# SSD scan of a two-layer hybrid backbone: decay tiles apart from their loads, convolutions written one tile ahead, other buffers in the first gates

## Chip, cores, metric

One Trainium2 chip; the kernel runs on one core. The metric is the time of one execution in device microseconds, the median of the runs shown.

## What is computed

Two layers over 1024 latent and 256 context tokens of width 1024: first a bidirectional Mamba-2 SSD mixer, then grouped-query attention, each followed by an expert-choice mixture of 16 SwiGLU experts. All inputs are float32. The change lies in the SSD mixer. What matters of it, from the reference:

```python
z, xbc, dtr = jnp.split(u @ in_w, [D_INNER, D_INNER + CONV_DIM], axis=-1)
xbc = jax.nn.silu(dwconv_centred(xbc, conv_w, conv_b))          # width 5, then x, B, C
dt = jax.nn.softplus(dtr.reshape(b, L, 2, SSD_HEADS) + dt_bias)
# per direction, chunks of 128 tokens, a = dt * A, acum = cumsum(a) in the chunk
seg = jnp.exp(jnp.where(tri, acum[..., :, None] - acum[..., None, :], -jnp.inf))
cb = jnp.einsum('bclgn,bcsgn->bcgls', Cc, Bc)                   # 8 groups, state size 128
y_diag = jnp.einsum('bcgrls,bcsgrp->bclgrp', cb[:, :, :, None] * seg, xdt)
states = jnp.einsum('bcsgn,bcgrs,bcsgrp->bcgrpn', Bc, decay_end, xdt)
# h[c+1] = chunk_decay[c] * h[c] + states[c]
y_off = jnp.einsum('bclgn,bcgrpn,bcgrl->bclgrp', Cc, h_prev, jnp.exp(acum))
y = y_f + flip(y_b) + D_skip * xs
out = rmsnorm(y * silu(z), norm_w) @ out_w
```

## The kernel before, in words

Work stands with channels on the 128 partitions and the 1280 tokens (10 chunks of 128, the first two are context) along the free dimension. Products of the projections are made from high and low halves of both factors (`mm3`, L51: three matmuls, L54 to L56).

The scan stage of `ssd` (from L303) runs over 8 groups (L501). A group has one B tile, one C tile and two x tiles of 128 channels (two heads each). Each of these is made by `conv_tile` (L333): the weights are fetched and split (`weights`, L306: the DMA on SP at L309, the high half on ACT at L311, the low half on POOL at L314), 72 projection matmuls of 256 or 512 columns go to `in_ps` (`proj`, L319, three PSUM buffers), ACT moves them out (L344, L345), and DVE makes the width-5 convolution and SiLU with four passes over 1284 columns (L349) and two over 642 (L354), with a tanh on ACT between them (L353). `cb` is the product of B and C by chunk (L513, moved out by ACT at L514). `transposed` (L357) turns B and x by chunk on PE (L363).

`core` (L384) is called for each of the two x tiles of a group (L519). It runs the backward states H1 (weighted x L370, matmul L396, the step on DVE L382), and then goes over five pairs of chunks. In round i of its loop pair i gets its `decays` (L403), that is the tile `Eb` with the log decays of both directions and heads (a DMA of 512 KB issued by SP at L405), masked by POOL (L408, two per pair), put through exp by ACT (L413, eight per pair); POOL adds the two directions in place (L416), DVE multiplies by `cb` (L417), and the result M is a view of the first half of `Eb`. `Eb` has three buffers. The same round takes pair i a step forward (`forward`, L420: L429, L382), makes the entering part of pair i-1 (`entering`, L435: matmuls L442, scaling on DVE L451, sum of directions on POOL L452, result `yos`), and the output of pair i-2 (`output`, L455: L460 with M, L463 with `yos`, both into `y_ps`; then L467 on DVE and the DMA of y to memory at L469).

Behind the scan the output gates follow: `gate` (L471) projects z for 128 channels, loads y back (L489) and multiplies (L490 to L492), writes the product (L493) and adds its squares (L499). The first two of sixteen (`early`, L524) are written while the pools of the scan are still held and take their tiles from `halves` (L529), two pairs out of the four quarters of one tile; the others take them from `pair` (L547).

The order of each engine's instructions is not that of the source. A scheduler takes the program as written, gives earlier written work precedence, and at each step places what its own estimate says is ready; buffers set when a tile can be used again. So the place at which a call stands sets how early its work may be placed, and work of a later tile fills what an earlier one leaves open.

## Time and profile before

| what | value |
|---|---|
| median of 3 runs (lowest to highest) | 3840.92 us (3840.58 to 3845.42) |
| the profiled execution, its own time | 3852.41 us |
| its span in the trace | 3850.6 us |
| PE busy (TensorE matmuls) | 3562.8 us, 93% |
| DVE / ACT / POOL busy | 2594.0 / 2024.8 / 1811.8 us |
| mean granted TensorE clock | 0.973 |

The span is divided by stage: the scan with its projections from about 142 to 992 us, the other gates and the output projection up to about 1470 us, the first mixture of experts, attention, the second mixture. PE is an engine whose work is pipelined, so that a busy stretch of it need not be PE at its peak; idle time of it and what ended it is read in the groups by line. In the rows, L12 is line 12 of the kernel before, `out<-in` are tiles, "128x512 f32<-128x512 f32" the shapes, and "x640" how many. The matmuls with float32 operands that the kernel writes as one stand as two instructions in the trace.

### The profile page before, as it was taken

The page shows a single profiled execution, that of the slowest core. Times are in us where ns is not written, and L with a number is a line of the kernel's source. Part 1 is how long each engine was busy: PE and PEld are TensorE (multiplying, and loading weights), DVE is VectorE, ACT ScalarE, POOL GpSimd, SP SyncE. Part 2 cuts the span into 40 slices and gives each one's busy share as a digit, 9 for nine tenths or more (in the row PEclk, how much of TensorE's full clock was granted, in tenths as well). Part 3 has the DMA queues.
Part 4 walks back from the last instruction along what each step waited for, and adds up shares of the span by engine and source line. Part 5 has one row for each costly group of instructions (what it writes and reads, how often), then busy time and mean ns, then how long its engine had stood idle before and what let it go on. Part 6 is the DMA issues. An engine that isn't in the chain of part 4 may idle for free.

```text
span 3850.6 us, 56599 instructions
## 1 busy us (share of the span) xinstructions
PE 3562.8 (93%) x21156; PEld 2674.7 (69%) x21156; DVE 2594.0 (67%) x3675; ACT 2024.8 (53%) x3310; POOL 1811.8 (47%) x1356
## 2 busy tenths in 40 slices
PE   6999999999898998999999998899999976999997
...
GB/s 191 108 104 116 128 90 83 79 77 90 161 137 142 119 117 244 315 305 311 319 320 304 287 238 91 39 17 1 1 1 12 118 168 265 371 382 379 343 339 163
DMA packets 296803, 681.10 MB, mean 177 GB/s; under 512 B 22568, under 2 KB 148400, under 8 KB 290384
## 3 DMA queue, kind: packets, MB, share of 16 engines
...
## 4 chain that ended last, share of the span: by engine, by line
PE 37%; DVE 11%; issue 6%; DMA 5%; POOL 4%; ACT 2%; SPq 0%; ACTq 0%; POOLq 0%; DVEq 0%
DVE m_w L728 6%; PE pv L1177 5%; PE S L1143 4%; PE a_tr L1164 4%; PE acc L54 4%; PE acc L56 4%; PE acc L55 4%; POOL m_w L725 3%; PE cacc L695 3%; DMA m_raw<-in_moe_w_dram 3%; PE o_ps L55 1%; PE o_ps L56 1%; PE o_ps L54 1%; PE qkv L56 1%; PE qkv L54 1%
## 5 line engine op out<-in xcount | busy, mean ns | idle before, releaser
L728 DVE TENSOR_TENSOR m_w<-m_raw,m_w 128x1792 fp32r<-128x1792 f32 (+1 forms) x384 | 890.5, 2342 | 251.8 <-ACT m_w L722 249.5
L722 ACT ACTIVATE m_w<-m_raw 128x2048 fp32r<-128x2048 f32 x384 | 732.6, 1916 | 485.9 <-DMA m_raw<-in_moe_w_dram 268.1
L725 POOL TENSOR_TENSOR m_w<-m_raw,m_w 128x256 fp32r<-128x256 f32 (+1 forms) x384 | 824.7, 2175 | 346.1 <-ACT m_w L722 343.5
L54 PE MATMUL in_ps<-hh,w 128*128 128x512 f32 (+1 forms) x1152 | 423.6, 368 | 7.7 <-DVE th L491 7.7
L55 PE MATMUL acc<-m_w,xl 128*128 128x512 f32 x1024 | 407.9, 399 | 22.3 <-DVE m_w L728 13.7
L56 PE MATMUL in_ps<-hh,w 128*128 128x512 f32 (+1 forms) x1152 | 420.7, 365 | 0.0
L55 PE MATMUL in_ps<-hl,w 128*128 128x512 f32 (+1 forms) x1152 | 418.7, 363 | 0.0
L54 PE MATMUL acc<-m_w,xl 128*128 128x512 f32 x1024 | 407.2, 404 | 4.5 <-ACT xl L48 4.5
L56 PE MATMUL acc<-m_w,xl 128*128 128x512 f32 x1024 | 402.1, 393 | 0.0
L413 ACT ACTIVATE Eb<-Eb,ebias 128x128 f32<-128x128 f32 x640 | 199.4, 391 | 165.2 <-POOL Eb L408 163.5
L1147 DVE TENSOR_REDUCE mx<-S 128x1 f32<-128x1024 f32 x128 | 155.7, 1216 | 181.2 <-PE S L1143 179.2
L1194 POOL TENSOR_TENSOR q<-s 64x128 f32<-64x128 f32 x128 | 58.7, 459 | 415.2 <-DVE mx L1152 347.4
L55 PEld LDWEIGHTS acc<-m_w,xl 128*128 128x128 f32 x1024 | 193.9, 189 | 83.9 <-DVE m_w L728 28.8
L54 PEld LDWEIGHTS in_ps<-hh,w 128*128 128x128 f32 x1152 | 220.1, 191 | 45.4 <-issue 10.9
L54 PEld LDWEIGHTS acc<-m_w,xl 128*128 128x128 f32 x1024 | 193.5, 190 | 69.6 <-issue 21.4
L56 PEld LDWEIGHTS in_ps<-hh,w 128*128 128x128 f32 x1152 | 220.0, 191 | 31.1 <-issue 5.0
L55 PEld LDWEIGHTS in_ps<-hl,w 128*128 128x128 f32 x1152 | 219.8, 191 | 29.2 <-issue 3.7
L314 POOL TENSOR_TENSOR w<-w_raw,w 128x512 fp32r<-128x512 f32 x96 | 154.5, 1630 | 166.4 <-ACT w L311 156.0
L56 PEld LDWEIGHTS acc<-m_w,xl 128*128 128x128 f32 x1024 | 193.7, 189 | 38.4 <-DVE xl L49 0.2
L55 PE MATMUL acc<-m_w,gT 128*128 128x512 f32 x512 | 204.4, 399 | 6.6 <-DVE m_w L728 4.1
L54 PE MATMUL acc<-m_w,gT 128*128 128x512 f32 x512 | 202.7, 402 | 1.0 <-ACT gT L48 1.0
L56 PE MATMUL acc<-m_w,gT 128*128 128x512 f32 x512 | 203.1, 397 | 0.0
...
## 6 DMA issues: line engine op xcount, KB each, us to landing
m_raw<-in_moe_w_dram SPq DMA_DIRECT2D x384, 1024.0 KB
...
```

What stands on the lines that cost most here:

```text
L54: mm(out, lhs[0], rhs[0], start=start, stop=False)
L55: mm(out, lhs[0], rhs[1], start=False, stop=False)
L56: mm(out, lhs[1], rhs[0], start=False, stop=stop)
L314: nc.gpsimd.tensor_tensor(w[1][:, sl], raw[:, sl], w[0][:, sl].bitcast(F32), op=OP.subtract)
L413: nc.scalar.activation(Eb[:, d, hh, cc], Eb[:, d, hh, cc], AF.Exp, bias=bias[:, c0 + cc, k:k + 1])
L722: nc.scalar.activation(w[0], raw, AF.Copy)
L725: nc.gpsimd.tensor_tensor(w[1][:, :, n:], raw[:, :, n:], w[0][:, :, n:].bitcast(F32), op=OP.subtract)
L728: nc.vector.tensor_tensor(w[1][:, :, :n], raw[:, :, :n], w[0][:, :, :n].bitcast(F32), op=OP.subtract)
L1143: nc.tensor.matmul(o, qTs[self.qt][:, 2 * self.hp + hh], kT[k][:, self.kv, 512 * b:512 * b + n], start=(k == 0), stop=(k == 1))
L1147: nc.vector.tensor_reduce(self.mx[:, 0:1], S[hh], axis=AX.X, op=OP.max)
L1164: nc.tensor.transpose(ps[:, q], self.pr[hh][:, (c0 + q) * P:(c0 + q + 1) * P], net.ident)
L1177: nc.tensor.matmul(self.pv[o:o + 64, 0], v32[:, t, self.kv], self.PT[:, t], start=(t < 2), stop=(t >= NT - 2))
```

## The change

- `decays` writes the sum of the two directions into a tile of its own, M, with three buffers, and `Eb` has two buffers in place of three.
- The calls are written in another order. `tile_BC` and `tile_x` hold the two kinds of convolution tile. B and C of group g+1 are written between the two cores of group g; both x tiles of a group are written ahead of its first core.
- The first two gates turn through all four quarters of one tile for y (`halves`), and take `th` from the buffers `raw` of the convolution.
- The 128x128 matrix of ones and the two triangles move from constants that are held all the time into the pool of the dt stage; the triangles are made by a memset and two affine selects on POOL in place of two comparisons on DVE. A column of ones stays.

```diff
--- before.py
+++ after.py
@@ -60,8 +60,7 @@
         nc, tc, A = self.nc, self.tc, self.A
         cp = self.cp = es.enter_context(tc.tile_pool(name="consts", bufs=1))
         self.ident = cp.tile([P, P], F32, name="ident")
-        self.tri = cp.tile([P, 2, P], F32, name="tri")
-        self.ones = cp.tile([P, P], F32, name="ones")
+        self.ones = cp.tile([P, 1], F32, name="ones")
         nc.vector.memset(self.ones, 1.0)
         self.eps = cp.tile([P, 1], F32, name="eps")
         nc.vector.memset(self.eps, EPS)
@@ -78,8 +77,6 @@
             nc.gpsimd.iota(jp, pattern=[[1, P]], base=0, channel_multiplier=-1,
                            allow_small_or_imprecise_dtypes=True)
             nc.vector.tensor_scalar(self.ident, jp, 0.0, None, op0=OP.is_equal)
-            nc.vector.tensor_scalar(self.tri[:, 0], jp, 0.0, None, op0=OP.is_ge)
-            nc.vector.tensor_scalar(self.tri[:, 1], jp, 0.0, None, op0=OP.is_le)
 
             r0 = pr.tile([P, P], F32, name="r0")
             r1 = pr.tile([P, P], F32, name="r1")
@@ -227,6 +224,13 @@
 
 
         with tc.tile_pool(name="dtp", bufs=1) as dp, tc.tile_pool(name="dtps", bufs=1, space=PSUM) as pp:
+            ones = dp.tile([P, P], F32, name="ones_pp")
+            tri = dp.tile([P, 2, P], F32, name="tri")
+            nc.vector.memset(ones, 1.0)
+            nc.vector.memset(tri, 1.0)
+            for d, sg in ((0, 1), (1, -1)):
+                nc.gpsimd.affine_select(tri[:, d], tri[:, d], pattern=[[sg, P]], base=0, channel_multiplier=-sg,
+                                        compare_op=OP.is_ge, fill=0.0)
             wdt = wp.tile([P, KT, P], F32, name="w_raw")
             nc.scalar.dma_start(wdt[:, :, 0:64], wv[:, :, 6144:6208])
             wdh = wp.tile([P, KT, 2, 64], F32R, name="w0")
@@ -279,9 +283,9 @@
             for d in range(2):
                 dsl = slice(32 * d, 32 * d + 32)
                 fps = pp.tile([P, NT, 32], F32, name="fps")
-                nc.tensor.matmul(fps, self.tri[:, d], a[:, :, dsl], start=True, stop=True)
+                nc.tensor.matmul(fps, tri[:, d], a[:, :, dsl], start=True, stop=True)
                 tps = pp.tile([P, NT, 32], F32, name="tps")
-                nc.tensor.matmul(tps, self.ones, a[:, :, dsl], start=True, stop=True)
+                nc.tensor.matmul(tps, ones, a[:, :, dsl], start=True, stop=True)
                 nc.vector.tensor_tensor(bias[:, :, dsl], ld[:, :, dsl], fps, op=OP.subtract)
                 nc.scalar.activation(eF[:, :, dsl], fps, AF.Exp)
                 fsb = dp.tile([P, NT, 32], F32, name="fsb")
@@ -293,7 +297,7 @@
             fr = dp.tile([64, NT, P], F32, name="fr")
             for t in range(NT):
                 rp = pp.tile([64, 2, P], F32, name="rps")
-                nc.tensor.matmul(rp, a[:, t, :], self.tri, start=True, stop=True)
+                nc.tensor.matmul(rp, a[:, t, :], tri, start=True, stop=True)
                 for d in range(2):
                     nc.scalar.activation(fr[32 * d:32 * d + 32, t], rp[32 * d:32 * d + 32, d], AF.Copy)
             for d in range(2):
@@ -401,7 +405,7 @@
             state = [None]
 
             def decays(c0):
-                Eb = co.tile([P, 2, 2, 2, P], F32, name="Eb", bufs=3)
+                Eb = co.tile([P, 2, 2, 2, P], F32, name="Eb", bufs=2)
                 nc.sync.dma_start(Eb.rearrange("p d h c l -> p (d h) (c l)"),
                                   rows(fd, [0, P], [TOK, 4], [1, 256], off=4 * ct * TOK + c0 * P))
                 for d, sg in ((0, 1), (1, -1)):
@@ -412,8 +416,8 @@
                             k = 32 * d + 2 * ct + hh
                             nc.scalar.activation(Eb[:, d, hh, cc], Eb[:, d, hh, cc], AF.Exp,
                                                  bias=bias[:, c0 + cc, k:k + 1])
-                M = Eb[:, 0]
-                nc.gpsimd.tensor_tensor(M, M, Eb[:, 1], op=OP.add)
+                M = co.tile([P, 2, 2, P], F32, name="M", bufs=3)
+                nc.gpsimd.tensor_tensor(M, Eb[:, 0], Eb[:, 1], op=OP.add)
                 nc.vector.tensor_tensor(M, M, cb[:, None, c0:c0 + 2].to_broadcast([P, 2, 2, P]), op=OP.mult)
                 return M
 
@@ -498,11 +502,22 @@
                     nc.scalar.activation(th[:, :n], yd[:, :n], AF.Square)
                     nc.gpsimd.tensor_tensor(acc[:, t0:t0 + n], first[:, t0:t0 + n], th[:, :n], op=OP.add)
 
-        for g in range(NG):
+        def tile_BC(g):
             BT = hp.tile([P, PTOK], F32, name="BT", tag="h_lo")
             CT = gp.tile([P, PTOK], F32, name="CT", bufs=2)
             conv_tile(16 + g, BT)
             conv_tile(24 + g, CT)
+            return BT, CT
+
+        def tile_x(ct):
+            xT = gp.tile([P, PTOK], F32, name="xT", bufs=2)
+            conv_tile(ct, xT)
+            return xT
+
+        BC = tile_BC(0)
+        for g in range(NG):
+            BT, CT = BC
+            xT = [tile_x(2 * g)]
             Btm = transposed(BT, "Btm", gp)
             cb = gp.tile([P, NT, P], F32, name="cb")
             for c0 in range(0, NT, 4):
@@ -512,10 +527,11 @@
                     sl = at(c0 + q)
                     nc.tensor.matmul(ps[:, q], BT[:, sl], CT[:, sl], start=True, stop=True)
                 nc.scalar.activation(cb[:, c0:c0 + n], ps[:, :n], AF.Copy)
-            for h in range(2):
-                xT = gp.tile([P, PTOK], F32, name="xT", bufs=2)
-                conv_tile(2 * g + h, xT)
-                core(2 * g + h, xT, CT, Btm, cb)
+            xT.append(tile_x(2 * g + 1))
+            core(2 * g, xT[0], CT, Btm, cb)
+            if g + 1 < NG:
+                BC = tile_BC(g + 1)
+            core(2 * g + 1, xT[1], CT, Btm, cb)
         for _ in mods:
             pass
 
@@ -526,8 +542,8 @@
 
         def halves():
             nonlocal turns
-            turns ^= 2
-            return zt[:, turns], zt[:, turns + 1]
+            turns = (turns + 1) % 4
+            return zt[:, turns], gp.tile([P, 1288], F32, name="raw", bufs=2)[:, :512]
         for ct in range(early):
             gate(ct, weights(ct * P), pin, halves, acc0, acc0 if ct else None)
         for p_ in (pst, ptp, pin, co, gp, adp, cs):
@@ -610,7 +626,7 @@
                     if t == NCT and h == 0:
                         ssp = pp.tile([P, NT], F32, name="r_lg")
                         for u in range(NT):
-                            nc.tensor.matmul(ssp[:, u:u + 1], self.acc[:, u * P:(u + 1) * P], self.ones[:, 0:1],
+                            nc.tensor.matmul(ssp[:, u:u + 1], self.acc[:, u * P:(u + 1) * P], self.ones,
                                              start=True, stop=True)
                         nc.scalar.activation(yr, ssp, AF.Sqrt, bias=self.eps, scale=1.0 / DI)
                         nc.vector.reciprocal(yr, yr)
```

What the scheduler makes of it is shown at three places. In the changed kernel the lines of `core` stand four later (L460 is L464, L463 is L467, L442 is L446, L417 is L421, L408 is L412, L382 is L386, L370 is L374, L349 is L353, L354 is L358, L452 is L456), the sum of directions is L420, and the matmul of cb L528.

First, PE at the fourth and fifth pair of a core's outputs in the steady part. Before:

```order
L442 MATMUL yo_ps<-H_7469,CT 128x128
L442 MATMUL yo_ps<-H_7254,CT 128x128
L55 MATMUL in_ps<-hl,w_7905 128x512
L56 MATMUL in_ps<-hh,w_7906 128x512
L54 MATMUL in_ps<-hh,w_7905 128x512
L55 MATMUL in_ps<-hl,w_7905 128x512
L56 MATMUL in_ps<-hh,w_7906 128x512
L54 MATMUL in_ps<-hh,w_7905 128x512
L55 MATMUL in_ps<-hl,w_7905 128x512
L460 MATMUL y_ps<-Eb,xtm 64x128 x2
L463 MATMUL y_ps<-ident,yos 128x128
```

and with the change, from the fourth pair's output to the fifth's:

```order
L467 MATMUL y_ps<-ident,yos 128x128
L367 MATMUL tr_ps<-ident,BT 128x128 x4
L54 MATMUL in_ps<-hh,w_5275 128x256
L55 MATMUL in_ps<-hl,w_5275 128x256
L56 MATMUL in_ps<-hh,w_5276 128x256
L464 MATMUL y_ps<-M,xtm 64x128 x2
L54 MATMUL in_ps<-hh,w_5275 128x256
L55 MATMUL in_ps<-hl,w_5275 128x256
L367 MATMUL tr_ps<-ident,BT 128x128 x2
L56 MATMUL in_ps<-hh,w_5276 128x256
L54 MATMUL in_ps<-hh,w_5275 128x256
L467 MATMUL y_ps<-ident,yos 128x128
```

Seven projections of 512 columns stood ahead of the fourth pair's output (and six ahead of the fifth's); now there are fewer and narrower ones, and the next group's B is turned between them.

Second, DVE around the convolution of C. Before:

```order
L349 SCALAR_TENSOR_TENSOR CT<-raw,pcol,CT 128x1284 x3
L354 SCALAR_TENSOR_TENSOR CT<-raw,CT 128x642 x2
L417 TENSOR_TENSOR Eb<-Eb,cb 128x512 x3
L349 SCALAR_TENSOR_TENSOR xT<-raw,pcol,xT 128x1284 x4
L354 SCALAR_TENSOR_TENSOR xT<-raw,xT 128x642 x2
L370 TENSOR_TENSOR xw_5247<-xtm,wst 128x256
```

and with the change:

```order
L353 SCALAR_TENSOR_TENSOR CT<-raw,pcol,CT 128x1284
L374 TENSOR_TENSOR xw_6896<-xtm,wst 128x256
L353 SCALAR_TENSOR_TENSOR CT<-raw,pcol,CT 128x1284
L382 COPY H_6895<-st_ps 128x128
L353 SCALAR_TENSOR_TENSOR CT<-raw,pcol,CT 128x1284
L386 SCALAR_TENSOR_TENSOR H_6895<-H_6895,dec,st_ps 128x64
L353 SCALAR_TENSOR_TENSOR CT<-raw,pcol,CT 128x1284
L386 SCALAR_TENSOR_TENSOR H_6895<-H_6895,dec,st_ps 128x64
L374 TENSOR_TENSOR xw_6904<-xtm,wst 128x512
L358 SCALAR_TENSOR_TENSOR CT<-raw,CT 128x642 x2
L386 SCALAR_TENSOR_TENSOR H_6895<-H_6895,dec,st_ps 128x64 x8
L374 TENSOR_TENSOR xw_6919<-xtm,wst 128x384
```

The C that stood right ahead of its use (cb, and through it L417) is now the C of the next group, between the backward states of this group's second core.

Third, POOL through a core's pairs (tiles yos, Eb and M). Before:

```order
L452 TENSOR_TENSOR yos<-yos 128x2x128 x2
L416 TENSOR_TENSOR Eb<-Eb 128x512
L408 AFFINE_SELECT Eb<-Eb 128x512 x4
L416 TENSOR_TENSOR Eb<-Eb 128x512
L452 TENSOR_TENSOR yos<-yos 128x2x128
```

and with the change:

```order
L456 TENSOR_TENSOR yos<-yos 128x2x128
L412 AFFINE_SELECT Eb<-Eb 128x512
L456 TENSOR_TENSOR yos<-yos 128x2x128
L412 AFFINE_SELECT Eb<-Eb 128x512 x3
L420 TENSOR_TENSOR M<-Eb 128x512
L456 TENSOR_TENSOR yos<-yos 128x2x128
```

The masks between the sums of yos are those of the next core's pairs now, and the last sum of yos of a core stands behind three of them and one sum into M.

## Rows read from the trace of the kernel before

**Rows 1.** The page of the profiled execution, its first part (busy time and share of the span of each engine) and the row of its second part for PE (40 slices of 96 us, busy share in tenths).

```profile
PE 3562.8 (93%) x21156; PEld 2674.7 (69%) x21156; DVE 2594.0 (67%) x3675; ACT 2024.8 (53%) x3310; POOL 1811.8 (47%) x1356
...
PE   6999999999898998999999998899999976999997
```

**Rows 2.** Busy time by window, us (number of instructions in brackets), for the whole scan stage and for one of its eight groups, from one group's first x transpose to the next one's; behind the engines the granted TensorE clock, the share of the DMA engines and GB/s.

```profile
142.00:992.00 850.00, 789.54 (x4804) 621.17 (x4804) 607.61 (x1130) 406.03 (x1012) 420.25 (x477) 0.99 0.32 101
705.00:811.50 106.50, 99.22 (x607) 80.40 (x605) 76.96 (x141) 52.04 (x129) 52.80 (x62) 0.98 0.26 82
```

**Rows 3.** Groups of PE instructions in the window 142 to 992 us: busy us, mean ns of one | idle time of PE before them and what ended it.

```profile
L442 PE MATMUL yo_ps<-H,CT 128*128 128x128 f32 x576 | 90.4, 279 | 0.2 <-DVE yos L451 0.2
L460 PE MATMUL y_ps<-Eb,xtm 128*64 128x128 f32 x640 | 86.3, 299 | 37.8 <-DVE Eb L417 18.2 <-issue 16.9 <-ACT Eb L413 1.8
L463 PE MATMUL y_ps<-ident,yos 128*128 128x128 f32 x320 | 74.8, 316 | 0.7 <-POOL yos L452 0.7
L429 PE MATMUL st_ps<-xw,Btm 128*128 128x128 f32 x288 | 59.0, 286 | 2.8 <-DVE H L382 2.3 <-DVE H L378 0.4
...
L363 PE MATMUL tr_ps<-ident,xT 128*128 128x128 f32 x160 | 27.8, 291 | 8.5 <-DVE xT L354 8.4
...
L513 PE MATMUL tr_ps<-CT,BT 128*128 128x128 f32 x140 | 20.3, 284 | 9.7 <-DVE CT L354 9.7
```

**Rows 4.** PE in order of time, the rows of that same group that have idle time before them (start, us, what, idle before it and its releaser).

```profile
777.58 0.44 PE L460 MATMUL y_ps<-Eb,xtm 128*64 128x128 f32 x4 [1.62 <-issue]
...
792.76 1.16 PE L513 MATMUL tr_ps<-CT,BT 128*128 128x128 f32 x8 [1.60 <-DVE CT L354]
...
811.08 0.63 PE L363 MATMUL tr_ps<-ident,xT 128*128 128x128 f32 x4 [0.99 <-DVE xT L354]
```

**Rows 5.** All engines in order of time, from the first pair's y of one core to the fourth pair's (SPq issues DMAs; rows of other work left out).

```profile
760.83 0.44 PE L460 MATMUL y_ps<-Eb,xtm 128*64 128x128 f32 x4
...
761.31 0.37 SPq L405 DMA_DIRECT2D Eb<-fd  x1
...
764.90 1.23 POOL L408 TENSOR_SCALAR_AFFINE_SELECT Eb<-Eb 128x512 f32<-128x512 f32 x2 [2.04 <-DMA Eb<-fd]
...
765.58 2.45 ACT L413 ACTIVATE Eb<-Eb,ebias 128x128 f32<-128x128 f32 x8 [2.12 <-POOL Eb L408]
...
768.52 0.72 POOL L452 TENSOR_TENSOR yos<-yos 128x256 f32<-128x256 f32 x1 [1.51 <-DVE yos L451]
...
769.20 1.28 POOL L416 TENSOR_TENSOR Eb<-Eb 128x512 f32<-128x512 f32 x1
...
769.86 1.97 DVE L349 SCALAR_TENSOR_TENSOR BT<-raw,pcol,BT 128x1284 f32<-128x1284 f32 x1
...
771.75 1.12 DVE L417 TENSOR_TENSOR Eb<-Eb,cb 128x512 f32<-128x512 f32 x1
...
772.93 0.44 PE L460 MATMUL y_ps<-Eb,xtm 128*64 128x128 f32 x4 [0.52 <-DVE Eb L417]
```

**Rows 6.** The tile Eb's instructions on POOL and DVE over the whole run: duration ns min/median/max, first and last start, forms.

```profile
L408 POOL TENSOR_SCALAR_AFFINE_SELECT Eb<-Eb x160: 632/640/1904, 153.8 to 981.0; 128x512 f32<-128x512 f32 x160
...
L416 POOL TENSOR_TENSOR Eb<-Eb x80: 1254/1288/2538, 158.1 to 984.2; 128x512 f32<-128x512 f32 x80
L417 DVE TENSOR_TENSOR Eb<-Eb,cb x80: 678/854/1775, 160.3 to 986.0; 128x512 f32<-128x512 f32 x80
```

**Rows 7.** Groups by shape on POOL in the window 142 to 992 us: busy us, mean ns of one | idle before.

```profile
L408 POOL TENSOR_SCALAR_AFFINE_SELECT Eb<-Eb 128x512 f32<-128x512 f32 x160 | 141.3, 900 | 64.5 <-DMA Eb<-fd 50.2 <-PE st_ps L429 9.5 <-PE tr_ps L363 2.5
L416 POOL TENSOR_TENSOR Eb<-Eb 128x512 f32<-128x512 f32 x80 | 123.6, 1548 | 16.7 <-ACT Eb L413 14.9 <-PE st_ps L396 1.6
...
L452 POOL TENSOR_TENSOR yos<-yos 128x256 f32<-128x256 f32 x64 | 50.8, 794 | 141.5 <-DVE yos L451 141.5
```

**Rows 8.** Groups by shape on DVE in the same window.

```profile
L349 DVE SCALAR_TENSOR_TENSOR xT<-raw,pcol,xT 128x1284 f32<-128x1284 f32 x63 | 111.6, 1772 | 32.6 <-ACT xT L345 31.7
...
L354 DVE SCALAR_TENSOR_TENSOR xT<-raw,xT 128x642 f32<-128x642 f32 x32 | 27.5, 882 | 8.9 <-ACT raw L353 8.9
L354 DVE SCALAR_TENSOR_TENSOR CT<-raw,CT 128x642 f32<-128x642 f32 x14 | 18.5, 1364 | 6.7 <-ACT raw L353 6.7
...
L370 DVE TENSOR_TENSOR xw<-xtm,wst 128x512 f32<-128x512 f32 x16 | 11.8, 738 | 2.5 <-ACT xtm L364 2.5
L370 DVE TENSOR_TENSOR xw<-xtm,wst 128x384 f32<-128x384 f32 x16 | 9.8, 610 | 0.0
```

**Rows 9.** DVE in order of time: eight H steps in a row, and a piece of a convolution.

```profile
749.12 1.62 DVE L382 SCALAR_TENSOR_TENSOR H<-H,dec,st_ps 128x64 f32<-128x64 f32 x8 [0.21 <-PE st_ps L396]
...
754.03 2.24 DVE L349 SCALAR_TENSOR_TENSOR BT<-raw,pcol,BT 128x1284 f32<-128x1284 f32 x1
```

**Rows 10.** PE in order of time: the first and the last of 25 projection matmuls of 512 columns in a row.

```profile
785.30 0.40 PE L54 MATMUL in_ps<-hh,w 128*128 128x512 f32 x1
...
790.77 0.39 PE L54 MATMUL in_ps<-hh,w 128*128 128x512 f32 x1
```

**Rows 11.** Busy time by window around the waits at 738.7 and 984.9 us, with the granted clock.

```profile
740.00:743.40 3.40, 3.40 (x13) 2.91 (x13) 1.52 (x4) 1.47 (x4) 2.12 (x6) 0.50 0.53 184
985.80:989.20 3.40, 3.40 (x14) 1.99 (x12) 2.88 (x4) 0.63 (x1) 0.83 (x2) 0.50 0.37 116
```

**Rows 12.** Groups of PE instructions in the window 992 to 1060 us, the first gates behind the scan.

```profile
L54 PE MATMUL in_ps<-hh,w 128*128 128x512 f32 (+1 forms) x96 | 36.3, 378 | 7.7 <-DVE th L491 7.7
```

## The prediction

> **What bounds the kernel now.** I read the page first, then busy time by window, then the groups of PE, then single waits in order of time. The first part of the page shows PE busy for 93% of the span; the slices show where the rest is, and that the scan is nowhere far below [rows 1]. The change touches the scan and the first gates alone. There PE is busy for 789.5 of 850 us, DVE for 607.6, POOL for 420.3 and ACT for 406.0 [rows 2]. So PE bounds the stage, and all that an order of instructions can give is PE's idle time there, 60.5 us. One group of the steady part takes 106.5 us, of which PE is idle for 7.3 [rows 2].
>
> The groups of PE tell who has this idle time [rows 3]: 37.8 us stand ahead of L460, the matmul that reads M; 9.7 ahead of L513 (cb) and 8.5 ahead of L363 (x turned), together 18.2, both ended by a last half of a convolution on DVE; and only 3.7 ahead of L429, L463 and L442. In a group's order of time one sees the pattern: the fourth pair's output waits 0.52, the fifth's 1.62, then cb 1.60 and the next x 0.99 [rows 4, 5].
>
> Why the fourth pair waits is to be read along one chain [rows 5]. The first pair's L460 starts at 760.83; its M is a view of Eb, so only then is a buffer free, and SP issues the load of the fourth pair's Eb at 761.31. The mask starts at 764.90, when it has landed; exp runs to 768.03; POOL's sum stands behind a sum of yos and ends at 770.48; DVE's product stands behind a piece of a convolution, runs from 771.75 to 772.87, and PE starts at 772.93. That is 12.1 us from one output to the next but two, and the seven projections between them don't cover it.
>
> **The change, part by part.**
>
> *Convolutions one tile ahead.* No instruction is added. In the new order 24 or more projections and most of a core lie between the last half of a convolution and the matmul that reads it, where about ten us lay before. Both waits were under 1.7 us each [rows 4]. Of the 18.2 us I take 17 as gone; the start of the first group keeps about one.
>
> *M in tiles of its own.* The sum costs the same: 512 columns in, 512 out, 1.548 us on POOL in the mean [rows 7]. What moves is when buffers come free. Eb is free after that sum, so its load, masks and exp for the next pairs run ahead of the outputs, up to two pairs; from the first pair's L460 to the fourth's M only the sum (1.3 to 1.5) and the product (1.1) are left, about 3 us with the hops, against 12.1. On SP the load of Eb stands ahead of the store of a y, as before, and waits for an earlier event than before. So the 37.8 us lose their cause. What takes their place comes from the new order on POOL and DVE.
>
> *The new waits.* (a) A core's last sum of yos now stands behind three masks and one sum into M, which belong to the next core: 3 x 0.900 + 1.548 + 0.794 = 5.0 us from the fourth sum's end to the fifth's [rows 7]. On PE there lie between the two outputs seven projections of 256 columns (half of 0.228 each, from 24 steps in 5.47 us [rows 10]: 0.8), six transposes (12 instructions of 27.8 / 160: 2.1), two L460 (four of 86.3 / 640: 0.5) and an L463 (two of 74.8 / 320: 0.5) [rows 3], in all 3.9. PE is short of cover by 1.1 us, if it comes to the fourth output together with POOL, and by nothing if POOL runs ahead. (b) Between the first weighted x of the backward states and the third DVE now has three convolution passes (3 x 1.772), two halves (2 x 0.882), two weighted x (0.738 + 0.610) [rows 8] and 11 small state operations (at 1.62 / 8 [rows 9]: 2.2), 10.6 us; PE has 34 projections of 512 columns (7.8), four of 256 (0.5) and ten small instructions (at 90.4 / 576: 1.6), 9.8. It is short by 0.8 at worst, and ahead of that PE has some 5 us of work against 4 of DVE. So a core's new waits lie between 0 and 1.9 us. I take 1.3, above the middle, because the means hide long single ones: masks of 1.904, sums of 2.538, products of 1.775 us [rows 6]. Over 16 cores that is +21; the ends are 0 and +30.
>
> *The clock.* The granted clock was 0.50, that is the lower level of 1.2 GHz, from 740.0 to 743.4 us, right behind a fifth pair's wait, and again from 985.8 [rows 11]; PE was fully busy in both, so each costs half of its 3.4 us. Both come behind waits that should go. I take 3 us back; the ends are 0 and 7, four such stretches.
>
> *First gates, constants.* With four quarters for y the loads of the first two gates stand earlier; their own waits are not among the larger ones, and the 7.7 us ahead of L54 behind the scan end at L491 of gates that take tiles from `pair`, unchanged [rows 12]. In the new order one projection instead of 17 stands behind the last output, so up to 3.6 us of cover (16 x 0.228) is lost at the turn to the next pools, or nothing, since two blocks of the next gate need no tile of them. I take 0, with 3.6 to either side. The masks of the triangles on POOL are done before PE's first use behind the whole dt chain: 0.
>
> **The sum:** -17 - 37.8 + 21 - 3 = -36.8 us. The profiled execution took 3852.4 us (span 3850.6), 11.5 above the median; from it the sum gives 3815.6, and from the median of 3840.9, which is what is compared, 3804.1. The forecast is **3804 us**.
>
> **A rule that speaks against it.** DVE's product takes from 678 to 1775 ns and POOL's mask from 632 to 1904 for equal work [rows 6], so the two engines slow each other. The Trainium skill, SBUF — State Buffer, section "Who interferes with whom", says why: a DVE instruction with two SBUF inputs and a GpSimd instruction that reads SBUF contend for one read interface, and one blocks fully while the other runs. The spread of rows 6 agrees. By that rule a shorter scan packs the same contending work closer, which is the last rival.
>
> **The rivals.**
>
> 1. *Only the convolution waits go.* The outputs wait as long as before, now for POOL's queue ((a) above) instead of the buffer. For it: POOL's masks of the next core stand ahead of the sums of yos in the new order, and 141.5 us of POOL's idle time already end at the product that yos needs [rows 7]. Against it: POOL is busy for half of the time [rows 2]. Time: 3840.9 - 17 = 3824.
> 2. *Nothing to tell.* New waits of about 3.3 us a core, 53 in all, where the upper end of the means is 1.9; the sum is then -17 - 37.8 + 53 = -2, that is 3839. It needs a slow pass in nearly each core.
> 3. *Slower: DVE falls behind in the backward states.* Place: between the first and the third weighted x, where convolution passes stand between the steps. If POOL's work falls on them so that a pass takes 2.24 [rows 9] and a half 1.364, as C's do now [rows 8], DVE needs 3 x 2.24 + 2 x 1.364 + 1.35 + 2.2 = 13.0 us against PE's 9.8, short by 3.2; with (a) doubled by the same contention, 2.6 more, a core waits 5.8 us, 93 in all. -17 - 37.8 + 93 = +38: 3879. It decides from 3.4 us a core upwards. Against it: DVE has 71% to do and rows of such length are the exception.
>
> **Chances and range.** About 0.2%, 7.7 us, is what a measurement can tell from no change. I give the forecast 0.48, the first rival 0.24, the second 0.15, the third 0.13. Faster by over 0.2% is then 0.72, within it 0.15, slower 0.13. The forecast's own range is 3786 (new waits near 0, the clock's 7 us, the turn 3.6 to the good: -17 - 37.8 - 7 - 3.6 and some 10 of waits) to 3818 (new waits of 30, clock 0, turn +3.6). The range for 8 in 10 reaches over both rivals up to no change: 3786 to 3842; it leaves out the third rival and a little below.
>
> **What would show it.** In the profile of the changed kernel the idle time ahead of the matmul of cb and of x turned should be under 2 us instead of 18.2, that ahead of the matmul with M under 15 instead of 37.8, PE's share of the scan near 96%, and a group near 102 us. Where new waits stand, they should be ahead of the matmul with yos, released by POOL, and ahead of the backward matmuls, released by a weighted x or a state step. The forecast is wrong if the idle time ahead of L464 stays near 30 us, or if that ahead of L467 and L400 together passes 40 us.

## The result and the profile after

The changed kernel takes **3898.68 us** (median of 4 runs, 3893.08 to 3906.48) against 3840.75 (4 runs, 3838.04 to 3845.42): a ratio of 1.0149, 95% interval 1.0136 to 1.0162. It is 58 us slower where 37 less were forecast.

The profiled executions stand 40.7 us apart (3893.1 and 3852.4). The last output of the scan ends at 1038.0 instead of 990.5 us, which is 47.5; from there to the last projection of the gates it takes 213.5 instead of 209.9, 3.6 more; the rest takes 2639.9 instead of 2650.2. That last part was long in the profiled execution of before (2636 to 2648 in the others below), which is most of what that one stood above its median. So nearly all of the loss is the scan's. Scan and gates make 51 of the 58 us; the profiled execution of the changed kernel was the fastest of its four, 5.6 us below their median, and the profile can't show what the others had more. Busy time by window, as in [rows 2]: the whole scan with its 4804 PE instructions, and one group of the steady part (us, number of instructions in brackets, then the granted clock, the DMA share, GB/s):

```profile
142.00:1040.00 898.00, 802.01 (x4804) 642.21 (x4803) 612.13 (x1128) 406.75 (x1011) 425.45 (x480) 0.96 0.30 94
745.50:858.80 113.30, 101.57 (x610) 83.91 (x608) 77.19 (x141) 52.72 (x129) 55.45 (x64) 0.95 0.26 77
```

The work is the same: the first column behind the length, PE, counts as many instructions as before, and DVE, ACT and POOL are as busy as before within 1.3%. PE's idle time grew from 60.5 to 96.0 us, its busy time from 789.5 to 802.0, and the mean granted clock fell from 0.99 to 0.96. A group takes 113.3 us, not 106.5. Who has the idle time, as in [rows 3]:

```profile
L446 PE MATMUL yo_ps<-H,CT 128*128 128x128 f32 x576 | 88.4, 278 | 4.8 <-DVE H L382 3.1 <-DVE yos L455 1.7
L464 PE MATMUL y_ps<-M,xtm 128*64 128x128 f32 x640 | 78.1, 308 | 1.7 <-DVE yd L471 1.6
L467 PE MATMUL y_ps<-ident,yos 128*128 128x128 f32 x320 | 77.7, 326 | 55.0 <-POOL yos L456 55.0
L433 PE MATMUL st_ps<-xw,Btm 128*128 128x128 f32 x288 | 59.6, 289 | 6.9 <-DVE H L386 5.8 <-DVE xw L374 0.6
L400 PE MATMUL st_ps<-xw,Btm 128*128 128x128 f32 x288 | 42.4, 284 | 6.7 <-DVE xw L374 6.6
L367 PE MATMUL tr_ps<-ident,xT 128*128 128x128 f32 x160 | 27.1, 285 | 15.6 <-ACT xtm L368 15.6
L528 PE MATMUL tr_ps<-CT,BT 128*128 128x128 f32 x150 | 26.3, 326 | 1.0 <-ACT cb L529 0.9
```

The waits that were to go did go: 37.8 us ahead of the matmul with M are 1.7, 9.7 ahead of cb are 1.0, and x turned no longer waits for a convolution. What came is larger: 55.0 ahead of L467 (0.7 before), 15.6 ahead of x turned, now for ACT, and 18.4 in the three groups of states. By pair of a core, L467's idle time is 0, 11.1, 2.1, 5.5 and 36.3 us. The largest of the fifth pair's waits, in order of time, PE with its projections left out:

```profile
715.20 0.49 PE L467 MATMUL y_ps<-ident,yos 128*128 128x128 f32 x2
715.52 0.60 PE L367 MATMUL tr_ps<-ident,BT 128*128 128x128 f32 x4
716.40 0.44 PE L464 MATMUL y_ps<-M,xtm 128*64 128x128 f32 x4
718.04 0.44 PE L367 MATMUL tr_ps<-ident,BT 128*128 128x128 f32 x2 [0.65 <-ACT Btm L368]
723.12 0.80 PE L467 MATMUL y_ps<-ident,yos 128*128 128x128 f32 x2 [4.53 <-POOL yos L456]
```

and POOL, then DVE, over the same stretch:

```profile
713.62 0.73 POOL L456 TENSOR_TENSOR yos<-yos 128x256 f32<-128x256 f32 x1
714.29 1.90 POOL L412 TENSOR_SCALAR_AFFINE_SELECT Eb<-Eb 128x512 f32<-128x512 f32 x1
716.14 0.10 POOL L342 MEMSET CT<- 128x4 f32 x1
716.19 2.48 POOL L412 TENSOR_SCALAR_AFFINE_SELECT Eb<-Eb 128x512 f32<-128x512 f32 x2
718.64 2.50 POOL L420 TENSOR_TENSOR M<-Eb 128x512 f32<-128x512 f32 x1
721.10 1.97 POOL L456 TENSOR_TENSOR yos<-yos 128x256 f32<-128x256 f32 x1
```

```profile
713.73 1.96 DVE L353 SCALAR_TENSOR_TENSOR xT<-raw,pcol,xT 128x1284 f32<-128x1284 f32 x1
...
716.01 0.68 DVE L455 TENSOR_TENSOR yos<-yo_ps,eF 128x512 f32<-128x512 f32 x1
716.61 3.40 DVE L353 SCALAR_TENSOR_TENSOR xT<-raw,pcol,xT 128x1284 f32<-128x1284 f32 x2
...
720.33 2.16 DVE L353 SCALAR_TENSOR_TENSOR xT<-raw,pcol,xT 128x1284 f32<-128x1284 f32 x1
```

This is place (a) of the prediction: the fifth pair's product is ready on DVE at 716.7, but its sum on POOL stands behind three masks and a sum into M of the *next* core. From the end of the fourth sum at 714.35 to the end of the fifth at 723.07 it is 8.7 us, and for 6.9 of them a convolution runs on DVE; PE has used up its work after 2.9 us (from 715.69 to 718.59). Over the first 15 cores the means are 6.5 us on POOL, 2.5 on PE, and a wait of 2.4; one to three masks stand in that stretch, three of them in six cores.

The kernel before had a stretch like it on POOL, from the fourth sum of yos of a core to the fifth:

```profile
768.52 0.72 POOL L452 TENSOR_TENSOR yos<-yos 128x256 f32<-128x256 f32 x1 [1.51 <-DVE yos L451]
769.20 1.28 POOL L416 TENSOR_TENSOR Eb<-Eb 128x512 f32<-128x512 f32 x1
770.43 2.94 POOL L408 TENSOR_SCALAR_AFFINE_SELECT Eb<-Eb 128x512 f32<-128x512 f32 x2
...
773.38 1.23 POOL L408 TENSOR_SCALAR_AFFINE_SELECT Eb<-Eb 128x512 f32<-128x512 f32 x2
774.96 1.29 POOL L416 TENSOR_TENSOR Eb<-Eb 128x512 f32<-128x512 f32 x1 [0.35 <-ACT Eb L413]
776.20 0.73 POOL L452 TENSOR_TENSOR yos<-yos 128x256 f32<-128x256 f32 x1
```

That is 7.7 us here and 6.8 in the mean of the first 15 cores, as long as now, and PE's own work between the two outputs was 2.4 us in the mean (2.3 now). Yet nothing waited for it, since POOL was ahead: the fourth sum is done at 769.24, and PE comes to the fourth output only at 772.93, behind projections and a wait for M ([rows 5]). In the mean the fourth sum ended 3.9 us before PE used it; in the changed kernel it is 0.5. So the length of that stretch is not new. What the change took away is POOL's head start.

Two groups of POOL in the scan of the changed kernel, as in [rows 7]:

```profile
L412 POOL TENSOR_SCALAR_AFFINE_SELECT Eb<-Eb 128x512 f32<-128x512 f32 x160 | 137.4, 880 | 103.2 <-DMA Eb<-fd 103.0
...
L456 POOL TENSOR_TENSOR yos<-yos 128x256 f32<-128x256 f32 x64 | 66.0, 1032 | 19.4 <-DVE yos L455 19.4
```

The masks are no slower in the mean, but the sum of yos is (1032 ns, 794 before). And of POOL's idle time only 19.4 us now end at the product that this sum needs, where 141.5 did. Before, POOL stood ready for two of a core's four products; now each of the four waits for POOL, 0.6 to 2.6 us in the mean.

Behind such waits the granted clock falls to half. Two of the stretches, at the waits that end at 499.2 and 723.1 us, by window:

```profile
499.90:503.30 3.40, 3.40 (x19) 3.32 (x16) 0.08 (x1) 0.78 (x2) 0.00 (x0) 0.50 0.62 185
721.80:728.60 6.80, 5.48 (x25) 4.93 (x26) 1.38 (x2) 0.89 (x2) 1.83 (x2) 0.50 0.32 96
```

A granted clock of 0.50 is the lower level, 1.2 GHz. The clock's records show 15 such stretches in the scan, 64.9 us together, each behind one or two waits of PE, mostly of 1.5 to 4.5 us; before there were four, 13.7 us ([rows 11] has two). A step from one projection of 512 columns to the next takes 0.43 us in the mean in these stretches, where it was 0.228 in [rows 10]. So the 51 us more at the lower clock are enough for the 12.5 us more of busy time that PE needs for the same instructions; no run separates the two.

Behind the scan the first gates wait 13.2 us where they waited 7.7 in [rows 12]; 3.6 of it is the turn to the next pools, which I had put at 3.6 to either side:

```profile
L54 PE MATMUL in_ps<-hh,w 128*128 128x512 f32 (+1 forms) x88 | 34.1, 387 | 13.2 <-DVE th L495 9.5 <-DVE yd L471 3.6
```

### The profile page after: what moved, and what is told of

The parts are those of the page before. It is cut to its first block, busy times and chain, and to the rows that moved or that the text cites. A ratio compares the mean times of both kernels' runs of the same rounds, so it can differ in the third digit from the quotient of the medians.

```text
span 3891.4 us, 56428 instructions
## 1 busy us (share of the span) xinstructions
PE 3575.1 (92%) x21156; PEld 2697.0 (69%) x21156; DVE 2603.2 (67%) x3675; ACT 2023.3 (52%) x3310; POOL 1810.5 (47%) x1358
## 4 chain that ended last, share of the span: by engine, by line
PE 36%; DVE 11%; issue 6%; DMA 4%; POOL 4%; ACT 2%; SPq 0%; ACTq 0%; POOLq 0%; DVEq 0%
DVE m_w L744 6%; PE pv L1193 5%; PE S L1159 4%; PE a_tr L1180 4%; PE acc L54 4%; PE acc L56 4%; PE acc L55 4%; PE cacc L711 3%; POOL m_w L741 3%; DMA m_raw<-in_moe_w_dram 3%; PE o_ps L55 1%; PE o_ps L56 1%; PE o_ps L54 1%; PE qkv L56 1%; PE qkv L55 1%
## 5 line engine op out<-in xcount | busy, mean ns | idle before, releaser
L54 PE MATMUL in_ps<-hh,w 128*128 128x512 f32 (+1 forms) x1152 | 428.0, 372 | 13.2 <-DVE th L495 9.5
L417 ACT ACTIVATE Eb<-Eb,ebias 128x128 f32<-128x128 f32 x640 | 202.5, 391 | 142.0 <-POOL Eb L412 138.1
L54 PEld LDWEIGHTS in_ps<-hh,w 128*128 128x128 f32 x1152 | 223.7, 194 | 54.3 <-DVE th L495 10.6
```

Of the source, the lines that this page charges most:

```text
L54: mm(out, lhs[0], rhs[0], start=start, stop=False)
L417: nc.scalar.activation(Eb[:, d, hh, cc], Eb[:, d, hh, cc], AF.Exp, bias=bias[:, c0 + cc, k:k + 1])
```

## The experiments

All runs in one table: the time, its ratio to the kernel before run beside it, and of the profiled execution PE's busy and idle time from 142 us to the end of the scan, and the scan's time at the lower clock. "New order" is the changed kernel. The runs were taken in sets, each beside runs of the kernel before, whose median was 3836.8 to 3842.0 us. So a difference between two runs is taken from their ratios, times 3840 us.

| run | us | ratio, 95% | PE busy | idle | lower clock |
|---|---|---|---|---|---|
| before | 3840.8 | 1 | 790 | 60 | 14 |
| changed | 3898.7 | 1.0149 (1.0136 to 1.0162) | 802 | 96 | 65 |
| e1 a first pair's masks behind | 3888.5 | 1.0139 (1.0113 to 1.0165) | 801 | 90 | 61 |
| e2 yos on DVE | 3877.1 | 1.0100 (1.0071 to 1.0130) | 796 | 84 | 65 |
| e3 old order | 3835.2 | 0.9995 (0.9984 to 1.0006) | 789 | 52 | 20 |
| e4 M in Eb, new order | 3856.1 | 1.0051 (1.0032 to 1.0070) | 800 | 68 | 68 |
| e5 only B, C ahead | 3869.3 | 1.0072 (1.0053 to 1.0092) | 805 | 72 | 78 |
| e6 only x ahead | 3871.6 | 1.0076 (1.0056 to 1.0096) | 799 | 78 | 44 |
| e7 old order, e1's edit | 3882.8 | 1.0098 (1.0080 to 1.0116) | 806 | 85 | 78 |
| e8 old order, yos on DVE | 3835.7 | 0.9985 (0.9974 to 0.9996) | 786 | 55 | 31 |
| e9 first x ahead | 3853.0 | 1.0035 (1.0022 to 1.0048) | 796 | 65 | 55 |
| e10 the same, yos on DVE | 3845.4 | 1.0013 (1.0002 to 1.0024) | 791 | 62 | 58 |
| e11 e1's edit, exps behind | 3877.8 | 1.0101 (1.0086 to 1.0117) | 791 | 83 | 17 |
| e12 wait filled | 3887.4 | 1.0129 (1.0113 to 1.0145) | 809 | 80 | 41 |
| e13 new order, no masks | 3839.4 | 1.0005 (0.9995 to 1.0015) | 793 | 58 | 44 |
| e14 old order, no masks | 3789.0 | 0.9869 (0.9854 to 0.9884) | 769 | 29 | 3 |
| e15 before, no masks | 3810.5 | 0.9929 (0.9914 to 0.9944) | 783 | 31 | 7 |
| e16 M alone | 3836.7 | 0.9993 (0.9984 to 1.0002) | 793 | 54 | 34 |

### Which part of the change it is: e3, e4, e5, e6, e16

e3 writes the calls of the scan as before, with M, early gates and constants as changed; e16 takes the early gates back too. e4 keeps the new order and makes M a view of Eb again:

```diff
-                Eb = co.tile([P, 2, 2, 2, P], F32, name="Eb", bufs=2)
+                Eb = co.tile([P, 2, 2, 2, P], F32, name="Eb", bufs=3)
...
-                M = co.tile([P, 2, 2, P], F32, name="M", bufs=3)
-                nc.gpsimd.tensor_tensor(M, Eb[:, 0], Eb[:, 1], op=OP.add)
+                M = Eb[:, 0]
+                nc.gpsimd.tensor_tensor(M, M, Eb[:, 1], op=OP.add)
```

e5 puts each x tile back right ahead of its own core and leaves B and C ahead; e6 the other way round:

```diff
 # e5
-            xT = [tile_x(2 * g)]
...
-            xT.append(tile_x(2 * g + 1))
-            core(2 * g, xT[0], CT, Btm, cb)
+            core(2 * g, tile_x(2 * g), CT, Btm, cb)
             if g + 1 < NG:
                 BC = tile_BC(g + 1)
-            core(2 * g + 1, xT[1], CT, Btm, cb)
+            core(2 * g + 1, tile_x(2 * g + 1), CT, Btm, cb)
 # e6
-        BC = tile_BC(0)
         for g in range(NG):
-            BT, CT = BC
+            BT, CT = tile_BC(g)
...
-            if g + 1 < NG:
-                BC = tile_BC(g + 1)
```

Expected of e3: 

> The changed kernel with the calls of the scan in the order of before (convolutions right ahead of their users); M in tiles of its own, Eb with two buffers, the early gates and the constants stay as changed. Queue theory: masks still run ahead of a last sum of yos in some cores, by one mask and a sum in place of three and a sum, so a smaller wait; the wait at L460 goes: 3815 to 3845 us. If M in tiles of its own with two buffers of Eb is the whole cause, 3880 us or more. If only the order is, 3840.9 - 38 = 3803 us.

Expected of e4: 

> The changed kernel with M as a view of Eb again and three buffers of Eb; the new order of calls, the early gates and the constants stay. Queue theory: Eb comes free only at the output, so no mask of the next core stands ahead of a last sum of yos by much; the outputs wait for Eb as before, the convolution waits go: 3820 to 3850 us. If the order alone makes the loss, 3880 us or more.

Expected of e5: 

> The changed kernel with only B and C of the next group written one tile ahead (between the cores); each x tile stands right ahead of its own core, as before. Theory of the x tiles (written ahead of the first core, they take the projections that stood between the waits and put two convolutions beside the first core's chain): at most 3850 us, idle time of PE in the scan near the 52 us of the old order, six to eight stretches at the lower clock. Theory of B and C (their convolutions between the backward states and beside the outputs do it): 3870 us or more.

Expected of e6: 

> The changed kernel with both x tiles of a group written ahead of its first core, but B and C at the head of their group, as before. Theory of the x tiles: 3875 us or more, twelve or more stretches at the lower clock. Theory of B and C: 3850 us or less.

Expected of e16: 

> M in tiles of its own and the constants moved; old order and old early gates. If the early gates cost or give nothing, the same as the third run, 3830 to 3840 us; if they cost the 2 to 3 us by which the gates behind the scan are longer, 3828 to 3834 us.

Measured: e3 3835 us, no difference from before; e16 the same, so the early gates neither cost nor give anything that can be told, and neither do M and the constants together in the old order. **The order of the calls makes the loss**, 59 us between e3 and the changed kernel. M in tiles of its own gives nothing in the old order, and in the new one it costs: e4 takes 38 us less than the changed kernel, and is still 20 us slower than before. The groups of PE in e3, and then in e4:

```profile
L464 PE MATMUL y_ps<-M,xtm 128*64 128x128 f32 x640 | 74.7, 301 | 0.0
L467 PE MATMUL y_ps<-ident,yos 128*128 128x128 f32 x320 | 74.7, 316 | 25.8 <-POOL yos L456 25.4
```

```profile
L464 PE MATMUL y_ps<-Eb,xtm 128*64 128x128 f32 x640 | 84.3, 314 | 45.9 <-DVE Eb L421 43.7 <-issue 1.8 <-DVE yd L471 0.2
L400 PE MATMUL st_ps<-xw,Btm 128*128 128x128 f32 x288 | 42.7, 282 | 11.4 <-DVE xw L374 11.4
```

In e3 the 37.8 us ahead of M are gone and 25.8 stand ahead of yos instead, 17.5 of them at the third pair, behind two masks of the next core and a sum into M of this one. With M apart the next core's masks run ahead in the old order too; but there they take 0.64 us and the sum 1.27, as nothing slows them at that place. In e4, whose time lay above the 3820 to 3850 us that the queue theory gave it, the conv waits are gone, the output waits longer than before, and the idle time is only 7 us more than before's, but in fewer, longer waits (up to 3.5 us), with 68 us at the lower clock and 10.6 more of busy time. Neither theory on the halves held: e5 lies between its 3850 and 3870 us and e6 between its 3850 and 3875. They cost 30 and 31 us over e3, 61 where both together cost 59. So it is not one of the tiles; either kind, written ahead, costs, and the two costs add up.

### Is it POOL's queue: e1, e2, e11, e7, e8

e1 was to put a core's masks behind the last sum of yos of the core before, e2 moves the sum to DVE, e11 adds to e1 that ACT's exps stand behind the move-outs of their own core's x:

```diff
 # e1
+            behind = sums[-1] if sums else None
...
+                    with tc.issue_after(behind.ins) if behind else nullcontext():
-                    nc.gpsimd.affine_select(Eb[:, d], Eb[:, d], ...)
+                        nc.gpsimd.affine_select(Eb[:, d], Eb[:, d], ...)
...
-                    nc.gpsimd.tensor_tensor(yos[:, :, 0], yos[:, :, 0], yos[:, :, 1], op=OP.add)
+                    sums.append(nc.gpsimd.tensor_tensor(yos[:, :, 0], yos[:, :, 0], yos[:, :, 1], op=OP.add))
 # e2
-                    nc.gpsimd.tensor_tensor(yos[:, :, 0], yos[:, :, 0], yos[:, :, 1], op=OP.add)
+                    nc.vector.tensor_tensor(yos[:, :, 0], yos[:, :, 0], yos[:, :, 1], op=OP.add)
 # e11: e1 and
+                            with tc.issue_after(moved.ins):
-                            nc.scalar.activation(Eb[:, d, hh, cc], Eb[:, d, hh, cc], AF.Exp,
+                                nc.scalar.activation(Eb[:, d, hh, cc], Eb[:, d, hh, cc], AF.Exp,
```

e7 is e1's edit and e8 e2's, each on e3. The edit of e1, e7 and e11 does only a part of what it was to do. `core` sets the name `behind` again in its loop over the pairs, so the masks of the first pair alone are held back; those of the second still go ahead. POOL in e1 at the end of a core shows it, two masks of the next core ahead of the last sum of yos and two behind it:

```profile
663.12 1.75 POOL L416 TENSOR_SCALAR_AFFINE_SELECT Eb<-Eb 128x512 f32<-128x512 f32 x2 [0.69 <-DMA Eb<-fd]
664.86 1.97 POOL L460 TENSOR_TENSOR yos<-yos 128x256 f32<-128x256 f32 x1
666.78 3.75 POOL L416 TENSOR_SCALAR_AFFINE_SELECT Eb<-Eb 128x512 f32<-128x512 f32 x2
```

In each of the first 15 cores of the changed kernel four masks of the next core stand ahead of that sum; in e1, e7 and e11 it is two.

Expected of e1: 

> The changed kernel, with the masks of a core (POOL) issued behind the last sum of yos of the core before; nothing else is moved by hand. Queue theory: the 36.3 us that PE stands ahead of the fifth pair's L467, and the stretches at the lower clock behind these waits (some 10 more than before, 1.7 us each), come from the three masks and the sum into M that stand ahead of that sum of yos. They go: 3840 to 3865 us, idle time ahead of L467 under 20 us. Density theory (convolutions and core packed closer make every pass on DVE, ACT and POOL late, and PE waits wherever the next one is): the wait moves to the next core's M or stays, 3885 us or more.

Expected of e2: 

> The changed kernel, with the sum of directions into yos on DVE in place of POOL (64 instructions of 128x256 out of POOL's queue into DVE's). Queue theory: L467 no longer stands behind masks, its idle time falls from 55 us to under 20, time 3840 to 3870 us, the 64 sums costing DVE some 0.4 us each beside other work. Density theory: DVE is the fuller engine (68% of the stage against POOL's 47%), so the outputs wait as long for it: 3890 to 3910 us.

Expected of e11: 

> The first run again (masks behind the last sum of yos of the core before), and ACT's exps of a core behind the move-outs of its own x turned, which PE waited for there (34.3 us ahead of the transposes of x). If each wait is a cost of its own: 34 us and their clock go, 3845 to 3860 us. If the delay only moves down the chain (to M, to the backward states): 3875 us or more.

Expected of e7: 

> The old order of calls with M in tiles of its own, and the masks of a core behind the last sum of yos of the core before (the two edits of the third and the first run together). Queue theory, now for the old order, where projections of the next x tile cover a late start of the next core: the 25.8 us ahead of L467 fall below 12 and nothing takes their place: 3815 to 3828 us. If the wait only moves to the next core's x, as in the new order, 3832 to 3840 us.

Expected of e8: 

> The old order of calls with M in tiles of its own, and the sum of yos on DVE. Queue theory: L467 no longer stands behind masks on POOL, its 25.8 us fall below 8; DVE's 64 sums of some 0.4 us lie beside projections: 3812 to 3826 us. If DVE is too full there, 3832 us or more.

Measured: e2 and e11 take 19 and 18 us less than the changed kernel; e1 takes 4 less, which can't be told from nothing. The queue theory had 34 to 59 for e1 and 29 to 59 for e2. Who PE waited for (us in total, times, longest), in e1:

```profile
PE tr_ps L367 <- ACT xtm L368: 34.3, 19, 3.2
PE y_ps L471 <- POOL yos L460: 25.9, 33, 3.2
```

in e2:

```profile
PE tr_ps L367 <- ACT xtm L368: 42.5, 12, 5.7
PE st_ps L433 <- DVE xw L374: 15.5, 12, 4.9
...
PE y_ps L467 <- DVE yos L456: 3.3, 7, 0.9
```

and in e11:

```profile
PE y_ps L473 <- POOL yos L462: 35.1, 31, 2.5
PE st_ps L404 <- DVE xw L374: 26.7, 28, 1.2
PE y_ps L470 <- DVE M L427: 8.2, 8, 1.7
```

The queue theory is right in its place: take half of the masks or the sum out of the way, and the fifth pair's L467 waits 10.6 us (e1, 25.9 for all pairs, where under 20 was expected) or 3.2 (e2) in place of 36.3. As an account of the time it falls, and of these two only e2 is a full test of it. The wait comes back further down. In e1 ACT's exps wait for the masks, and behind them in ACT's queue stands the move-out of the next core's x; PE, which needs that, stands still for 3.21 us up to 683.69:

```profile
678.10 3.91 ACT L421 ACTIVATE Eb<-Eb,ebias 128x128 f32<-128x128 f32 x13 [3.83 <-POOL Eb L416]
...
683.05 0.58 ACT L368 ACTIVATE xtm<-tr_ps 128x512 f32<-128x512 f32 x1
```

In e2, where no mask was moved, the longest wait of this kind (5.7 us, to 676.90) also stands behind exps, and these behind two masks that waited for their load:

```profile
670.76 1.62 POOL L412 TENSOR_SCALAR_AFFINE_SELECT Eb<-Eb 128x512 f32<-128x512 f32 x2 [3.15 <-DMA Eb<-fd]
```

With the exps behind the move-outs (e11), PE waits for the weighted x and for the next outputs. Idle time stays between 83 and 90 us. In the old order e1's edit even costs (e7 40 us over e3, where no cost was expected); e8 is the only run with masks whose interval lies below 1, by 0.15%, which is less than a measurement here can tell, with 20.9 us now ahead of cb.

### What the order costs without the masks: e13, e14, e15

These three leave the masks out, so the decays above the diagonal are not set aside, and have tanh in place of exp; ACT is busy in the scan for 405 to 408 us, as it is with exp (406 to 408).

```diff
-                    nc.gpsimd.affine_select(Eb[:, d], Eb[:, d], pattern=[[0, 2], [0, 2], [sg, P]], base=0,
-                                            channel_multiplier=-sg, compare_op=OP.is_ge, fill=MASKED)
...
-                            nc.scalar.activation(Eb[:, d, hh, cc], Eb[:, d, hh, cc], AF.Exp,
+                            nc.scalar.activation(Eb[:, d, hh, cc], Eb[:, d, hh, cc], AF.Tanh,
```

Expected of e13: 

> The changed kernel without the 160 masks on POOL (left out: the decays above the diagonal are not set aside; tanh stands in place of exp on ACT, so that values stay finite). Masks theory (POOL's masks beside DVE's convolutions make the chains late): idle time of PE in the scan falls from 94 us below 40, and the new order shows its gain over the old one without masks: 3800 to 3830 us. DVE theory (the convolutions in DVE's queue are enough): idle time stays over 65 us, 3860 us or more.

Expected of e14: 

> The same two edits on the kernel with the old order and M in tiles of its own, as the control. Masks theory: 3805 to 3825 us, more than the new order without masks takes, by the conv waits of 14 us that only the new order covers. DVE theory: less than the new order without masks by 30 us or more.

Expected of e15: 

> The same two edits on the kernel before (M a view of Eb, three buffers). The chain from one output to the next but two is shorter by the two masks (1.2 of 12.1 us) and by what stands behind them: the 37.8 us ahead of its output halve, 3815 to 3830 us on either theory; it shows what masks cost where nothing else was changed.

Measured: the masks hold 55 us of the time in the new order, 48 in the old one with M apart, 27 in the kernel before. So the masks theory has a share. But the new order costs 52 us over the old one without any mask too, as the DVE theory said (30 or more). Of e13 itself neither theory had the time (3839 us lies between 3830 and 3860) or the idle time (58 us, between 40 and 65). e15 lies below the 3815 to 3830 us expected: the wait ahead of its output with M fell from 37.8 to 6.0 us and not to half. The fifth pair of one core in e13, POOL and then DVE:

```profile
641.87 2.22 POOL L418 TENSOR_TENSOR M<-Eb 128x512 f32<-128x512 f32 x1 [0.28 <-ACT Eb L415]
644.39 2.18 POOL L418 TENSOR_TENSOR M<-Eb 128x512 f32<-128x512 f32 x1 [0.30 <-ACT Eb L415]
646.53 1.17 POOL L454 TENSOR_TENSOR yos<-yos 128x256 f32<-128x256 f32 x1
```

```profile
641.01 1.93 DVE L353 SCALAR_TENSOR_TENSOR BT<-raw,pcol,BT 128x1284 f32<-128x1284 f32 x1
...
643.25 0.68 DVE L453 TENSOR_TENSOR yos<-yo_ps,eF 128x512 f32<-128x512 f32 x1
643.86 1.59 DVE L353 SCALAR_TENSOR_TENSOR BT<-raw,pcol,BT 128x1284 f32<-128x1284 f32 x1
645.37 1.75 DVE L419 TENSOR_TENSOR M<-M,cb 128x512 f32<-128x512 f32 x1
```

The product is there at 643.93; the sum of yos begins at 646.53, behind two sums into M that wait for ACT and take 2.2 us beside a convolution of the next group's B. The pattern is the same without masks: work of the next core ahead of the last sum of this one, slowed by convolutions that the new order put there. From the end of the second pair's output to the end of the fifth's, DVE spends 5.9 us a core in convolutions in the changed kernel and 3.0 in e3 (4.6 in e13, 2.4 in e14, means of the first 15 cores). That is not all of it: e5, 30 us slower than e3, has 3.2. And M in tiles of its own is worth 23 us (e15 to e14) once the masks are out of its way.

### A smaller step, and the clock: e9, e10, e12

e9 keeps only the first x of a group ahead of cb; the second goes back behind the first core. e10 adds e2's edit. e12 repeats two matmuls right ahead of the wait:

```diff
 # e9, from e6
-            xT.append(tile_x(2 * g + 1))
             core(2 * g, xT[0], CT, Btm, cb)
+            xT.append(tile_x(2 * g + 1))
 # e12
-                    for hh in range(2):
+                    for hh in list(range(2)) * (6 if c == NT - 2 else 1):
```

Expected of e9: 

> Between the old and the new order: B and C at the head of their group and the group's first x right behind them, ahead of cb, as in the new order; the second x right ahead of its own core, as in the old. Only the wait for C's and B's last halves is covered, and no tile that a later core needs is written ahead of a core. If it is the tiles written ahead of a core that cost (their projections, ACT's move-outs and DVE's passes take part in that core's chain): 3820 to 3838 us, cb's wait under 2 us, at most six stretches at the lower clock. If M's early masks alone cost, whatever the order: 3860 us or more.

Expected of e10: 

> The same order with the sum of yos on DVE. In the old order with that sum on DVE, 20.9 us stood ahead of cb and 0 to 2 us ahead of L467; if both repairs add, 3812 to 3830 us. If what leaves one wait comes back at the next (the group's chain through DVE is as long as PE's work), 3832 us or more.

Expected of e12: 

> The changed kernel with the two L464 of the first chunk of a core's fifth pair done six times over, right ahead of the L467 that waits (20 more instructions of the trace a core, some 0.11 us each, 2.2 us; their result is the same). PE works where it stood idle for 36.3 us over the cores. If the lower clock behind the waits costs time of its own, fewer stretches at it follow and the time falls by 5 to 15 us, to 3884 to 3894 us; if only the waiting itself counts, the time stays or rises by what stands outside of a wait, 3898 to 3910 us.

Measured: e9 takes 3853, above the 3820 to 3838 us expected if only tiles written ahead of a core cost, with 12 stretches at the lower clock, where six at most were expected; 42.0 us stand ahead of L467 again, so my account by tiles written ahead of a core is not the whole one. In e10 they are 2.1, and 23.9 ahead of B turned and 27.1 ahead of x turned have taken their place. e12 does 320 more instructions and yet takes 8 us less than the changed kernel, though the intervals of the two ratios overlap, so that this much is not sure: 16 us less idle and 41 in place of 65 us at the lower clock pay for the added work. That fits a share of the clock in the loss but doesn't size it. The four runs of e11 go the same way, 3865.3 us at a mean clock of 0.973 and 3876.0 to 3882.3 at 0.967 to 0.969; the 17 us in the table belong to the first of them, so they are low for e11.

## Why the prediction was wrong, point by point

- **Conv waits, -17.** The idle time ahead of cb fell by 8.7 and that ahead of x turned ended its wait for DVE, as said. But x turned now waits 15.6 us for ACT, whose move-out stands behind exps and other move-outs. I costed no queue of ACT's.
- **Waits for M, -37.8.** Right in size and cause: 36.1 went (and all in e3). That they were a gain was wrong: what takes their place comes from the order on POOL, which I said, and is as large, which I did not.
- **New waits, +21: the step that failed.** They were put at 1.3 us a core with ends of 0 and 1.9. Measured are 87 us, 5.5 a core, and the prediction's own sign of being wrong came: L467 and L400 together have 61.7 us, where 40 was the limit. Term (a) was mis-sized on both sides. On POOL the stretch took 6.5 us where I added 5.0 from means over the whole scan. PE's cover was 2.5 where I added 3.9, and most of that is a slip in counting: a transpose stands as one instruction in the trace, not as two, so the six are 1.0 us (0.60 and 0.44 in the rows above) and not 2.1. So 1.1 us short became 4.0, and a wait of 2.4 in the mean. I also let POOL run ahead in the better case, without asking what had kept it ahead before: PE's waits for M, 2.4 us a core, gave it a part of its head start of 3.9 us, and the change removes them. And I priced L467 for the fifth pair alone; the second to fourth have 18.7. Term (b) held in its place: L400 has 6.7 us, 0.4 a core, within 0 to 0.8. The forward states (L433, L446), which I put at nothing, have 8.7 us more than before, and x and B turned, for ACT, have 17.6.
- **Why POOL was slow at that place.** In the changed kernel an instruction with a convolution pass on DVE beside it for at least a quarter of its time takes 1.30 us for a mask (0.71 otherwise), 2.17 for a sum into M (1.31), 1.51 for a sum of yos (0.78). I used means in which most were undisturbed. At the disturbed durations the term is 3 x 1.30 + 2.17 + 1.51 = 7.6 us, above the 6.5 measured, since not all were beside a convolution. By the Trainium skill, SBUF — State Buffer, section "Who interferes with whom", a DVE instruction with two SBUF inputs and a GpSimd instruction that reads SBUF share a read interface, and one blocks. The durations above agree. Over the whole scan POOL was not slower for it: only the sum of yos was, with 22 of 64 beside a convolution where it was 8 before.
- **Clock, -3.** The sign was wrong. The stretches at the lower clock went from 13.7 to 64.9 us, and PE's busy time rose by 12.5. I counted those behind waits that go, not those behind waits that come.
- **First gates and constants, 0 ± 3.6.** At the edge of it: the profile has 3.6 more, and e16 against e3 shows nothing.
- **The range.** Its upper end was added up wrong: -17 - 37.8 + 30 + 3.6 is -21.2, from the median 3819.7 and not 3818. Nothing hangs on it.
- **The rivals.** The slower rival had the right sign, the right cause (POOL beside convolutions) and, by chance, nearly the right price (5.8 us a core, 5.5 measured); its place was wrong, since the backward states hold 6.7 us and the outputs 55.0. The first rival had the place: the outputs wait for POOL's queue now. I let that end only in a smaller gain.

The sum by measured terms: -36.1 (M) - 8.7 (cb) - 8.5 (x, for DVE) + 55.0 - 0.7 (L467) + 15.6 (x, for ACT) + 18.4 - 3.0 (states) + 12.5 (busy time) is 44.5. With 2.0 ahead of B turned and a rest of 1.0 it gives the 47.5 us by which the scan is longer.

**What stays open.** Why each repair moves the wait on by nearly its whole length is not settled. It would be so if the chain of a core through DVE, POOL and ACT sets the pace and PE's projections are already spent there; no run gave PE more of them at that place. A rival that no run tests is the number of buffers of Eb, two with M apart and three without: of POOL's idle time 103.0 us end at a load of Eb in the changed kernel, 64.5 before ([rows 7]), and e4 takes back the third buffer together with M. Nor did a run hold back all masks of the next core, since e1's edit reaches half of those that stood ahead. Nor is it settled why PE's busy time in e14 is 20 us below that of before, where only 10 us less are at the lower clock.
